# A two-block kernel with another order of its second block, a joint compression and longer value-product runs

## The chip, the cores and the metric

One core of a Trainium2 chip runs the whole program in one launch. The metric is the device time of one execution in microseconds (us). TensorE (PE) does matrix products and transposes, VectorE (DVE), ScalarE (ACT) and GpSimd (POOL) the elementwise work, and SyncE (SP) issues nearly all DMAs. PEld is the weight-load side of TensorE: a matmul's stationary operand is loaded there while an earlier matmul still runs.

## What is computed

The input is 512 tokens of 1024 features, in float32. Two transformer-like blocks follow one another. The reference, cut to what matters here:

```python
def reference(x, ...):
    x = first_block(x, ...)
    return second_block(x, ...)

# first_block
    xn = rms_norm(h, mix_norm[l])
    proj = jnp.einsum("bsd,dp->bsp", xn, w_in[l]) + b_in[l]
    q, k, v, cb, cc, cx, ga, gc = jnp.split(proj, splits, axis=-1)
    attn = sliding_window_attention(q, k, v, sinks[l])
    conv = cb * causal_depthwise_conv(cc * cx, conv_w[l])
    merged = (jax.nn.sigmoid(ga) * jnp.einsum("bsc,cd->bsd", attn, w_attn_branch[l])
              + jax.nn.sigmoid(gc) * jnp.einsum("bsc,cd->bsd", conv, w_conv_branch[l]))
    h = h + jnp.einsum("bsd,de->bse", merged, w_out[l])
    # then h = h + feed-forward part, with a depthwise convolution, and rms_norm

# second_block
    h = x @ w_in[l]                       # 33 projections of up to 128 columns
    o_nsa = nsa_mixer(...)                # 6 heads: compressed, selected and window branch
    o_sb = stick_breaking_mixer(...)      # 4 heads
    o_hg = hgrn2_mixer(...)               # 6 heads, a gated recurrence
    mixed = jnp.concatenate([o_nsa * silu(nsa_z), o_sb * silu(sb_z), o_hg * silu(hg_z)], axis=-1)
    x = layer_norm(ALPHA * x + mixed @ w_out[l], ln_g[l], ln_b[l])

# nsa_mixer
    def compress(src, w1, w2):            # src: keys or values, 31 blocks of 32 tokens
        blocks = src[:, blk_idx] + cmp_pos
        return gelu(blocks.reshape(..., 32 * dk) @ w1) @ w2
    kc, vc = compress(kc_src, w_ck1, w_ck2), compress(vc_src, w_cv1, w_cv2)
    # each branch: softmax(q k^T + bias) v, then
    return gb[..., 0:1] * o_c + gb[..., 1:2] * o_s + gb[..., 2:3] * o_w
```

## The kernel before, in words

**Tiling.** Features lie on the 128 partitions and the 512 tokens on the free axis. A dense projection (`dense`, L218) makes one 128x512 tile from 8 blocks of 128 input features. Float32 is split in a high and a low part, so that each block costs three matmuls of 512 columns: high weights times high and low input (`wh`), low weights times high input (`wl`); 24 matmuls for a projection. The weights of a projection come as one 512 KB DMA into `raw` (two buffers), ScalarE casts them to `wh` (L196), VectorE subtracts to get `wl` (through `tt`, L136). `Weights.take` has the load four projections ahead of use and the splitting two ahead.

**The stages**, in time from the start of the span: the first block's 34 input projections with its attention (12 to 165 us), branches and output (165 to 272), the feed-forward part (272 to 673), and the second block: 33 projections (673 to 1007), during which all of its three mixers run, then the transposes of the residual (to 1014) and the output products (1015 to 1060).

**Streams in the second block.** The mixers are Python generators that emit instructions and yield estimated costs. `drive` (L165) always advances the stream that stands lowest in cost divided by its rate: the projections (`in_proj2`, rate 1), `stream_a` (recurrences and stick-breaking heads one after another as in `SEQ`, slowed by `RATE_A`), `sparse` (compression, then the 24 units of the sparse attention, slowed by `RATE_B`) and `finishing` (the products with the gates). `ORDER` is the order of the 33 projections and `KORD` that of the last eight, the gates z. Each engine runs its instructions in the order so emitted, apart from places marked with a priority: weight splitting is lifted by 100 places, and `run` (L141) emits a list of matmuls as one block that waits for all of its inputs.

**Names.** Projections: `gf gq gi` of the recurrence (three pairs of heads), `nq` the sparse queries (three pairs), `kc vc` the keys and values to compress, `ks vs kw vw` those of the selected and window branches, `ng` their gates, `bq bk bv` the stick-breaking heads (two pairs). PSUM tiles: `pm` two banks for dense work, `pga` and `pgb` two each for scores and transposes, `poa` and `pob` one each for results. SBUF tiles are named by pools of 128x512 buffers: `nk`, `dk`, `hk`, `lv`, `np`, `gp`, `bi`, `r`.

**Matmul shapes.** Heads are 64 wide. Value products put the two heads of a pair in the two column halves of TensorE (`128*64` in the rows: 64 output partitions), all other products use its whole width (`128*128`).

**Compression before.** `compress` (L840) is called for keys and again for values: four loads of 256 KB bring the first weight `w1` into `nk` tiles, 8 additions on VectorE (L857) build the blocks, and 16 float32 matmuls with `w1` stationary and 62 columns moving (31 blocks of two groups) make the hidden layer, followed by a gelu on small tiles. `compressed` (L882) then applies `w2`, and for each of 4 query tiles makes scores of 6 heads with 31 keys, in float32, a softmax, and transposes. The results are `kcT` and `vcn`.

**One unit of the sparse attention before** is a pair of heads j, a query tile i and a branch br: `nsa_a` makes scores and softmax (L942, L948, L955), and while the next unit's scores are emitted `nsa_b` (L958) transposes the probabilities into `pgb` (L965), copies them to SBUF (L967, one on VectorE, one on ScalarE), and emits the value products into `pob` as one `run` (the compressed branch's two products go with br 0). The first block's attention (`softmax_a`, `softmax_b`, L457 and L493) works in the same way for units (j, ip), with one run of value products for each.

## Time and profile before

| | |
|---|---|
| time, median of 3 runs | 1068.86 us (1068.28 to 1069.32) |
| the profiled execution's own time | 1068.53 us |
| its span | 1066.8 us |
| granted TensorE clock, mean | 0.999 |
| TensorE busy | 1039.5 us, 97% |
| VectorE busy | 704.4 us, 66% |
| ScalarE busy | 488.8 us, 46% |
| GpSimd busy | 44.0 us, 4% |

1.7 us of the profiled time lie outside the span. Busy time is the union of an engine's records; a TensorE record's end is modelled and reaches past the start of the next one, so that "busy" tells that work is queued, not that the array runs at its peak. What a matmul costs in a row of others is read from the distance of starts. A wait of PEld can still be covered by a matmul that runs; idle time of PE cannot.

### The profile page before, as it was taken

What the parts mean: (1) busy time and instruction counts of PE and PEld (TensorE: products, weight loads), DVE (VectorE), ACT (ScalarE), POOL (GpSimd) and SP (SyncE); (2) the same over time, 40 slices, a digit from 0 to 9 for tenths busy, and PEclk for the clock granted to TensorE, in tenths of its full rate; (3) what the DMA queues carried; (4) which work ended last, traced back from release to release, by engine and by line L of the source; (5) the groups of instructions that cost most, each with busy time, mean ns of one, the idle gap of its engine ahead of it and who ended that gap; (6) DMA issues with size and microseconds to landing.
All of it is one profiled execution on the core that took longest, in us unless ns stands there. A gap on an engine that the chain in (4) does not pass through costs nothing.

```text
span 1066.8 us, 14636 instructions
## 1 busy us (share of the span) xinstructions
PE 1039.5 (97%) x5712; PEld 838.9 (79%) x5712; DVE 704.4 (66%) x1313; ACT 488.8 (46%) x855; POOL 44.0 (4%) x89
## 2 busy tenths in 40 slices
PE   8999999999999999999999999999999999989997
PEld 6788888888888888888877888767777777767886
DVE  6876643356448777777763233597967698887757
ACT  5754443322344444444442222433625676578740
POOL 0000000000220000000000111200000000011000
PEclk9999999999999999999999999999999999999999
DMA  6212232333432233223335333531321110101232
GB/s 218 79 60 80 79 94 85 99 99 109 142 120 85 98 99 99 98 99 99 99 94 193 97 106 90 184 101 41 99 75 47 59 41 22 41 21 37 82 120 79
DMA packets 32801, 97.84 MB, mean 92 GB/s; under 512 B 4878, under 2 KB 5390, under 8 KB 32732
## 3 DMA queue, kind: packets, MB, share of 16 engines
q1 hardware_dynamic: 32732, 96.91, 28.7%
q8 instruction: 45, 0.74, 0.3%
q14 instruction: 24, 0.20, 0.1%
HBM read 94.77 MB, written 5.27 MB: 94 GB/s over the span
## 4 chain that ended last, share of the span: by engine, by line
PE 75%; DVE 11%; ACT 7%; DMA 3%; issue 2%; SPq 1%; POOL 1%; DVEq 0%; POOLq 0%; ACTq 0%
PE pm L139 44%; PE pob L139 12%; PE poa L139 12%; PE pga L139 4%; PE pgb L139 3%; DVE wl L136 2%; DMA raw<-in_w_in 1%; ACT wh L196 1%; DVE lv L136 1%; DMA raw<-in_w_down 1%; DVE hk L136 1%; DVE dk L136 1%; DVE np L136 1%; DVE nk L942 1%; ACT nk L948 1%
## 5 line engine op out<-in xcount | busy, mean ns | idle before, releaser
L139 PE MATMUL pm<-x,wh 128*128 128x512 f32 (+1 forms) x1360 | 433.4, 395 | 2.1 <-DVE x L133 0.9
L139 PEld LDWEIGHTS pm<-x,wh 128*128 128x128 f32 (+1 forms) x1360 | 252.2, 187 | 58.5 <-issue 3.5
L196 ACT CAST wh<-raw 128x1024 fp32r<-128x1024 f32 (+1 forms) x153 | 156.7, 1025 | 275.8 <-issue 109.9
L139 PE MATMUL pm<-x,wl 128*128 128x512 f32 (+1 forms) x680 | 268.3, 395 | 0.0
L136 DVE TENSOR_TENSOR wl<-raw,wh 128x1024 fp32r<-128x1024 f32 (+1 forms) x153 | 181.9, 1189 | 89.5 <-ACT wh L196 87.7
L139 PEld LDWEIGHTS pm<-x,wl 128*128 128x128 f32 (+1 forms) x680 | 127.0, 187 | 26.8 <-issue 1.6
L139 PE MATMUL poa<-x,wh 128*128 128x512 f32 x208 | 65.0, 394 | 0.0
L139 PE MATMUL pob<-x,wh 128*128 128x512 f32 x208 | 64.1, 390 | 0.0
L139 PE MATMUL pm<-np,wh 128*128 128x512 f32 x176 | 54.1, 389 | 0.0
L136 DVE TENSOR_TENSOR dk<-pm,rs 128x512 f32<-128x512 f32 x43 | 29.5, 686 | 28.1 <-PE pm L139 28.0
L139 PEld LDWEIGHTS poa<-x,wh 128*128 128x128 f32 x208 | 39.0, 188 | 9.3 <-issue 1.0
L139 PEld LDWEIGHTS pob<-x,wh 128*128 128x128 f32 x208 | 39.0, 188 | 8.0
L136 DVE TENSOR_TENSOR nk<-pm,rs 128x512 f32<-128x512 f32 x34 | 23.4, 687 | 32.6 <-PE pm L139 32.4
L139 PE MATMUL poa<-x,wl 128*128 128x512 f32 x104 | 40.6, 390 | 0.1
L139 PE MATMUL pob<-x,wl 128*128 128x512 f32 x104 | 40.6, 390 | 0.0
L139 PEld LDWEIGHTS pm<-np,wh 128*128 128x128 f32 x176 | 33.0, 188 | 6.8
L139 PE MATMUL pm<-np,wl 128*128 128x512 f32 x88 | 34.2, 389 | 0.0
L948 ACT ACTIVATE nk<-nk,q 128x128 f32<-128x128 f32 (+3 forms) x48 | 26.5, 555 | 11.5 <-DVE q L946 11.2
L942 DVE CUSTOM_DVE_ANT_0 nk<-pgb,bi 128x128 f32<-128x128 f32 (+3 forms) x48 | 23.1, 484 | 7.9 <-PE pgb L139 7.2
L133 DVE SCALAR_TENSOR_TENSOR dk<-nk,smt,dk 128x511 f32<-128x511 f32 (+1 forms) x34 | 25.4, 748 | 1.4 <-ACT dk L435 0.8
L139 PE MATMUL pgb<-np,np 128*128 128x128 f32 (+3 forms) x96 | 25.9, 351 | 0.4 <-DVE nk L967 0.3
L133 DVE SCALAR_TENSOR_TENSOR nk<-nk,smt,nk 128x511 f32<-128x511 f32 (+2 forms) x33 | 24.7, 747 | 0.5
(498 smaller groups left out, 1664.7 us busy)
## 6 DMA issues: line engine op xcount, KB each, us to landing
raw<-in_w_in SPq DMA_DIRECT2D x65, 512.0 KB, 3.5
raw<-in_w_up SPq DMA_DIRECT2D x44, 512.0 KB, 3.5
raw<-in_w_down SPq DMA_DIRECT2D x16, 512.0 KB, 3.6
raw<-in_w_br SPq DMA_DIRECT2D x8, 512.0 KB, 3.4
raw<-in_w_out SPq DMA_DIRECT2D x8, 512.0 KB, 3.5
raw<-in_w_out SPq DMA_DIRECT2D x16, 256.0 KB, 2.7
raw<-in_w_down SPq DMA_DIRECT2D x8, 384.0 KB, 3.2
d<-d SPq DMA_DIRECT2D x6, 512.0 KB, 6.6
```

The costliest lines, as they stand in the source:

```text
L133: V.scalar_tensor_tensor(o, i0, s, i1, op0, op1)
L136: V.tensor_tensor(o, i0, i1, op)
L139: return TE.matmul(o, l, r, start=start, stop=stop)
L196: A.copy(wh[:, c], raw[:, c])
L942: V.tensor_tensor_reduce(pb[:, 0:Wd_], s[:, 0:Wd_], bias[h][:, T - Wd_:T], 1.0, -3e38, ALU.add, ALU.max, st[:, g:g + 1])
L948: A.activation(pbs[g][:, 0:Wd_], pbs[g][:, 0:Wd_], AF.Exp, bias=st[:, 2 + g:3 + g], accum_out=st[:, 4 + g:5 + g])
```

## The change

1. **Order.** `ORDER`, `KORD` and the driver are new. `in_step` takes the projections as a clock (5.2 units of cost are one projection), and each stream has a first and a last projection in `PLAN` between which its cost is spread evenly. The three pairs of the sparse attention (`sparse(j)`) are three streams now, and the finishing steps come as streams at the end.
2. **Compression.** `blocks` (in place of `compress`) brings the weights, now into `np` tiles, and builds the blocks; `compressed` does the hidden layer of keys and values together: the block columns are stationary (64 wide), `w1` moves with 128 columns, keys go to the lower and values to the upper column half, 32 matmuls in one `run`. The gelu is done once on 128x128, and a transpose brings the result back. The compressed keys are kept split as high and low part side by side (`kc2`, 62 wide), and the scores use the queries' high and low parts as fp32r, all six heads of a query tile in one PSUM bank, with one more addition on VectorE.
3. **Value products.** `nsa_c` emits those of both branches and the compressed one in one `run` for each (j, i): 12 runs for 24. `softmax_c` does the same for the two units of a pair in the first block: 4 runs for 8. The copies of the first block now go to `lv` tiles, and some gates and merged tiles lie in other pools for that.

The diff, cut to its core:

```diff
-RATE_A = [0.593, 0.587, 0.591, 0.741, 0.778]
-RATE_B = [0.318, 0.367, 0.286, 0.332, 0.497]
-ORDER = [('gf', 0), ('gq', 0), 'kc', ('gi', 0), 'ng', 'vc', ('nq', 0), ('gf', 1), ('gq', 1), ('nq', 2), 'kw', 'ks', 'vs', ('bq', 0), ('gi', 1), ('gf', 2), 'vw', ('bk', 0), ('nq', 1), ('bv', 0), ('gq', 2), ('gi', 2), ('bq', 1), ('bk', 1), ('bv', 1)]
-KORD = [6, 5, 7, 0, 3, 1, 4, 2]
+ORDER = [("gf", 0), ("gq", 0), ("gi", 0), "ng", "kc", "vc", ("nq", 0), ("nq", 1), ("nq", 2), "ks", "vs", "kw", "vw",
+         ("gf", 1), ("gq", 1), ("gi", 1), ("bq", 0), ("bk", 0), ("bv", 0), ("gf", 2), ("gq", 2), ("gi", 2),
+         ("bq", 1), ("bk", 1), ("bv", 1)]
+PLAN = {("g", 0): (3, 9), ("g", 1): (16, 20), ("b", 0): (19, 24), ("g", 2): (23, 28), ("b", 1): (27.5, 32.5),
+        "c": (6, 12.5), ("n", 0): (13, 19.5), ("n", 1): (19.5, 26), ("n", 2): (26, 32.5)}
+KORD = [3, 0, 1, 5, 6, 7, 4, 2]
...
+    def in_step(clock, *streams):
...
+            for s in sorted(live, key=lambda s: s[3] + (s[4] - s[3]) * s[1] / s[2]):
+                g, did, work, first, last = s
+                if running and now < first + (last - first) * did / work:
+                    break
...
+                now += c / 5.2
...
-    def softmax_b(j, ip, po, sbs, lo):
+    def softmax_b(j, ip, sbs, lo):
...
-            pT = wk()
+            pT = tl("lv")
...
+    def softmax_c(po, held):
+        todo = []
+        for i, sblk, hh, w, first, last in held[0][0] + held[1][0]:
+            r = 64 * hh
+            todo.append(later(po[r:r + 64, i * P:(i + 1) * P], vn[:, sblk * P + r:sblk * P + r + 64], w, first, last))
+        run(todo, held[0][1] + held[1][1])
+        yield 2.0
...
-    def compress(name, w1name, w2name):
-        w1 = [nk().rearrange("p (k h) -> p k h", k=4) for _ in range(4)]
+    def blocks(name, w1name, w2name):
+
+        w1 = [np_().rearrange("p (k h) -> p k h", k=4) for _ in range(4)]
...
-        for k in range(16):
-            mm(ps[:, 0:62], w1[k // 4][:, k % 4], blks[k // 8][:, 62 * (k % 8):62 * (k % 8) + 62], k == 0, k == 15)
...
+        wk1, wk2, bk, e0 = yield from blocks("kc", "w_ck1", "w_ck2")
+        wv1, wv2, bv, e1 = yield from blocks("vc", "w_cv1", "w_cv2")
+
+        ps = bank("gb")
+        todo = []
+        for k in range(16):
+            c = slice(62 * (k % 8), 62 * (k % 8) + 64)
+            for r, w1, blks in ((0, wk1, bk), (64, wv1, bv)):
+                todo.append(later(ps[r:r + 64, 0:P], blks[k // 8][:, c], w1[k // 4][:, k % 4], k == 0, k == 15))
+        run(todo, [e0, e1])
...
+        TE.transpose(ps[:, 0:P], y, ident)
+        A.copy(yT, ps[:, 0:P])
...
+        A.copy(kc2[:, :, 0:31], kv)
+        tt(kc2[:, :, 31:62], kv, kc2[:, :, 0:31].bitcast(F32), ALU.subtract)
...
-                    mm(ps[:, 32 * h:32 * h + 31], pr["nq", h][g][:, i * P:(i + 1) * P].bitcast(F32), kcT[:, g, 0:31])
-                tt(pv[:, 3 * g:3 * g + 3], ps[:, 0:96].rearrange("p (h n) -> p h n", n=32)[:, :, 0:31],
-                   biasc[i][:, 3 * g:3 * g + 3], ALU.add)
+                    n = 64 * (3 * g + h)
+                    mm(ps[:, n:n + 62], pr["nq", h][g][:, i * P:(i + 1) * P], kc2[:, g, 0:62])
+            sv = ps[:, 0:384].rearrange("p (h n) -> p h n", h=6)
+            tt(pv, sv[:, :, 0:31], biasc[i], ALU.add)
+            tt(pv, pv, sv[:, :, 31:62], ALU.add)
...
+    def nsa_c(j, i, po, held):
+
+        todo, ends = [], []
...
+        for br, (pts, e) in enumerate(held):
+            vn_ = pr[("vs", "vw")[br]]
+            ends += e
+            for b in range(i + 1):
+                for g in range(2):
+                    r = 64 * g
+                    todo.append(later(po[r:r + 64, i * P:(i + 1) * P], vn_[:, b * P + r:b * P + r + 64],
+                                      pts[g][:, b * P:(b + 1) * P], False, br == 1 and b == i))
         run(todo, ends)
-        yield 0.16 * (i + 1)
...
-    drive((in_proj2(), 1.0), (stream_a(), 1.0), (sparse(), 1.0), (finishing(KORD), 1.0))
+    plan = [((recurrence if kind == "g" else sticks)([c]), 12.6 if kind == "g" else 13.2, *PLAN[kind, c])
+            for kind, c in SEQ]
...
+    in_step(in_proj2(), *((chain(n), *plan[n][1:]) for n in range(len(SEQ))),
+            (compressed(), 6.8, *PLAN["c"]), *((sparse(j), 14.2, *PLAN["n", j]) for j in range(3)),
+            *((finishing(n), 1.0, len(ORDER) - 8.0, len(ORDER) + 0.0) for n in KORD))
```

What this does to the instructions is seen from how they stand on an engine. On TensorE, before, a unit of the sparse attention late in the second block: the transposes of the probabilities (`pgb<-cst,nk`), a few dense matmuls of a projection (`pm<-x`), scores of a later unit (`pgb<-np,np`), then the value products of branch 1 alone (`pob<-nk,np`, 64 wide). `nk_7469` and `nk_7476` are the copies of the two transposes.

```order
L965 MATMUL pgb_7464<-cst,nk_7154 128x128 x4
L139 MATMUL pm_8245<-x_4420,wh_8169 128x512
L965 MATMUL pgb_7471<-cst,nk_7159 128x128 x4
L139 MATMUL pm_8245<-x_4419,wl_8170 128x512
L139 MATMUL pm_8245<-x_4511,wh_8169 128x512
L139 MATMUL pm_8245<-x_4512,wh_8169 128x512
L139 MATMUL pgb_7766<-np_5941,np_5902 128x128
L139 MATMUL pgb_7766<-np_5943,np_5902 128x128
L139 MATMUL pm_8245<-x_4511,wl_8170 128x512
L139 MATMUL pob_6944<-nk_7469,np_6434 64x128
L139 MATMUL pob_6944<-nk_7476,np_6434 64x128
```

Six matmuls stand there between the second transpose and the products that need its copy; the products of branch 0 stood in a run of their own earlier.

On TensorE, after, a unit with two key blocks (query tile i = 1): the end of the last transposes, dense matmuls, then one run with the compressed products (`np,vcn`), those of branch 0 (`np_6002`) and of branch 1 (`np_6115`).

```order
L1020 MATMUL pgb_6332<-cst,nk_6241 128x128 x2
L141 MATMUL pm_6339<-x_4883,wl_6272 128x512
L141 MATMUL pm_6339<-x_4976,wh_6271 128x512
L141 MATMUL pm_6339<-x_4977,wh_6271 128x512
L141 MATMUL pob_6124<-np_5901,vcn_5082 64x128 x2
L141 MATMUL pob_6124<-nk_6284,np_6002 64x128
L141 MATMUL pob_6124<-nk_6289,np_6002 64x128
L141 MATMUL pob_6124<-nk_6284,np_6002 64x128
L141 MATMUL pob_6124<-nk_6289,np_6002 64x128
L141 MATMUL pob_6124<-nk_6330,np_6115 64x128
L141 MATMUL pob_6124<-nk_6335,np_6115 64x128
```

One run stands for two, and the copies of branch 0 (`nk_6284`, `nk_6289`), whose transposes stand some 25 rows higher, have another unit's scores and many dense matmuls behind them.

The other place is the compression, TensorE again. Before, keys: 16 float32 matmuls of 62 columns into one bank, in two halves with dense matmuls of the next projection (`pob<-x`) between, and the same again for values.

```order
L139 MATMUL pgb_5297<-nk_5287,nk_5151 128x62 x4
L139 MATMUL pgb_5297<-nk_5287,nk_5152 128x62 x4
L139 MATMUL pob_5341<-x_4697,wl_5258 128x512
L139 MATMUL pob_5341<-x_4790,wh_5257 128x512
L139 MATMUL pob_5341<-x_4791,wh_5257 128x512
```

After, keys (`np_5577` is their `w1`) and values (`np_5599`) alternate in the two halves of one run.

```order
L141 MATMUL pgb_5623<-np_5577,nk_5587 64x128
L141 MATMUL pgb_5623<-np_5599,nk_5611 64x128
L141 MATMUL pgb_5623<-np_5577,nk_5587 64x128
L141 MATMUL pgb_5623<-np_5599,nk_5611 64x128
L141 MATMUL pgb_5623<-np_5577,nk_5587 64x128
```

The run now stands as one piece of 32 matmuls, behind all 16 block additions. On SyncE's DMA queue, after, the loads of `w1` come ahead of the bias tiles (`bi`) and of the third projection's weights (`raw_5102`); before, the bias loads stood directly behind `raw_5100`, and `raw_5102` behind them.

```order
L220 DMA raw_5098<-in_w_in 128x1024
L884 DMA np_5577<-in_w_ck 128x512
L884 DMA np_5578<-in_w_ck 128x512
L220 DMA raw_5100<-in_w_in 128x1024
L884 DMA np_5579<-in_w_ck 128x512
L884 DMA np_5580<-in_w_ck 128x512
L884 DMA np_5599<-in_w_cv 128x512
L884 DMA np_5600<-in_w_cv 128x512
L861 DMA bi_5085<-d_4300 128x512
```

Six loads of 256 KB have moved ahead of `raw_5102`, and each `np` tile that they write must first be released by TensorE.

## Rows read from the trace of the kernel before

**Rows 1.** The page's engine summary: busy time, share of the span, instructions.
```profile
PE 1039.5 (97%) x5712; PEld 838.9 (79%) x5712; DVE 704.4 (66%) x1313; ACT 488.8 (46%) x855; POOL 44.0 (4%) x89
```
**Rows 2.** The view by stretches: busy time of engines, PEclk the granted clock.
```profile
core 0: us, PE busy (x) PEld busy (x) DVE busy (x) ACT busy (x) POOL busy (x), PEclk, DMA share, GB/s
673.00:690.00 17.00, 16.17 (x70) 12.73 (x69) 9.25 (x18) 9.23 (x14) 6.80 (x27) 1.00 0.64 213
690.00:1003.00 313.00, 300.85 (x2301) 232.09 (x2300) 255.13 (x626) 183.58 (x389) 12.10 (x34) 1.00 0.17 54
...
940.00:980.00 40.00, 35.12 (x234) 25.47 (x234) 30.85 (x81) 32.91 (x75) 7.04 (x16) 1.00 0.09 27
```
**Rows 3.** PEld's waits, 690 to 1003 us: total us, times, longest; 8 of 27 rows.
```profile
PEld pob L139 <- ACT nk L967: 7.4, 18, 1.2
PEld pgb L139 <- issue: 4.5, 20, 1.1
...
PEld pgb L965 <- DVE q L942: 2.8, 7, 0.5
PEld pm L139 <- issue: 2.7, 12, 0.3
PEld pgb L139 <- DVE nk L857: 2.5, 3, 1.4
...
PEld pgb L377 <- DVE dk L136: 1.9, 1, 1.9
...
PEld pgb L965 <- DVE nk L955: 1.6, 5, 0.5
...
PEld pgb L925 <- issue: 0.4, 1, 0.4
```
**Rows 4.** PE matmuls by shape, 670 to 1005: count, busy, mean ns, idle before.
```profile
L139 PE MATMUL pob<-nk,np 128*64 128x128 f32 x240 | 17.8, 278 | 0.1
...
L139 PE MATMUL pgb<-nk,nk 128*128 128x62 f32 x64 | 8.2, 278 | 2.1 <-DVE nk L857 1.3 <-issue 0.8
...
L139 PE MATMUL pgb<-kcT,np 128*128 128x31 f32 x48 | 6.2, 261 | 0.1
```
**Rows 5.** Timeline of PE, 694 to 703: start, duration; x16 is sixteen records.
```profile
695.33 2.00 PE L139 MATMUL pgb<-nk,nk 128*128 128x62 f32 x16 [0.95 <-DVE nk L857]
697.13 0.48 PE L139 MATMUL pob<-x,wl 128*128 128x512 f32 x1
...
697.91 0.39 PE L139 MATMUL pob<-x,wl 128*128 128x512 f32 x1
698.14 0.62 PE L139 MATMUL pob<-x,wh 128*128 128x512 f32 x2
```
**Rows 6.** Timeline, 929 to 935: copies of transposes and the run behind them.
```profile
931.46 0.68 DVE L967 COPY nk<-pgb 128x512 f32<-128x512 f32 x1
...
932.37 0.56 ACT L967 COPY nk<-pgb 128x512 f32<-128x512 f32 x1
...
932.98 0.85 PEld L139 LDWEIGHTS pob<-nk,np 128*64 128x64 f32 x16 [0.38 <-ACT nk L967]
932.99 1.09 PE L139 MATMUL pob<-nk,np 128*64 128x128 f32 x16
```
**Rows 7.** Timeline of PE, residual transposes: fp32r matmuls of 128 columns.
```profile
1010.82 0.61 PE L139 MATMUL pm<-trir,x 128*128 128x128 f32 x4
1011.26 0.61 PE L139 MATMUL pgb<-trir,x 128*128 128x128 f32 x4
```
**Rows 8.** The chain of waits at the second block's start: start, duration.
```profile
673.45 6.29 DMA raw<-in_w_in
...
680.91 1.23 DVE wl L136
```
**Rows 9.** Timeline of PE, 685 to 688: the first matmul of the third projection.
```profile
686.28 0.62 PE L139 MATMUL pm<-x,wh 128*128 128x512 f32 x2
```
**Rows 10.** PEld's waits, 36 to 130 us, the first block's attention.
```profile
PEld poa L139 <- ACT nk L503: 0.9, 2, 0.4
```

More of the change, by code (lines that the diff above doesn't have):

```diff
@@ L159, in need @@
             yield None
-    def paced(g, rate):
-        for c in g:
-            yield c if c is None else c / rate
+    def in_step(clock, *streams):
+        now = 0.0
+        live = [[g, 0.0, work, first, last] for g, work, first, last in streams]
+        running = True
+        while running or live:
+            moved = False
+            for s in sorted(live, key=lambda s: s[3] + (s[4] - s[3]) * s[1] / s[2]):
+                g, did, work, first, last = s
+                if running and now < first + (last - first) * did / work:
+                    break
+                try:
+                    c = next(g)
+                except StopIteration:
+                    live.remove(s)
+                    moved = True
+                    break
+                if c is None:
+                    if did == 0:
+                        s[3] = max(first, min(now, last - 1.0))
+                    continue
+                s[1] += c
+                moved = True
+                break
+            if moved:
+                continue
+            if not running:
+                raise RuntimeError("nothing can go on")
+            try:
+                c = next(clock)
+                while c is None:
+                    c = next(clock)
+                now += c / 5.2
+            except StopIteration:
+                running = False
     def drive(*tasks):
@@ L1001, in sparse @@
             prev = (un, new)
+        o = rt()
+        A.copy(o, po)
+        outs[j] = o
+        done.add(("nsa", j))
     ZP = [(0, 0), (1, 0), (2, 0), (1, 384)]
```

136 lines of the change are left out of this document (62 added, 74 removed).

## The prediction

> **What bounds the kernel now.** I read the engine summary first [rows 1]: TensorE is busy 1039.5 of 1066.8 us, VectorE 66%, the others less. So the time falls only by what leaves TensorE's stream, as work or as waiting. Then the view by stretches [rows 2], since the change touches mainly the second block: from 690 to 1003 us TensorE is busy 300.85 of 313 us at a granted clock of 1.00, so the clock gives nothing, and 12.15 us are idle by its own records. VectorE has 255 us of work there, ScalarE 184. Then the waits of the weight loads in the same stretch [rows 3]. Its rows that name another engine sum to 35.4 us (27 rows in all, the first, the last and six more shown) and those marked "issue" to 11.1 us. Both measures are bounds: a late weight load is partly covered by the matmul that still runs, and a matmul's modelled end hides part of an idle gap. So TensorE loses between 12 and 35 us to waits on other engines there; I use the middle, 24. The largest is the value product behind the copy of its transposed probabilities (7.4 us in 18 waits). The timeline shows why [rows 6]: the copies end at 932.14 and 932.93, the loads of the products had waited 0.38 us and start at 932.98.
>
> **The compression.** The 62-column float32 run starts at 695.33 and the next dense matmul at 697.13 [rows 5]: 1.80 us for 8 matmuls (16 records, since float32 makes two passes), 0.225 each. The group counts 64 records, so 32 matmuls [rows 4], 7.2 us. Afterwards 32 matmuls of 128 columns in two column halves. The form exists in the trace as the value product: 16 records take 1.09 us, one lasts 0.278 [rows 4, 6], so starts are (1.09 - 0.278) / 15 = 0.054 apart, 0.108 a matmul: 32 cost 3.5 us. The added transpose is one 128-column pass or two, 0.1 to 0.2. Together -3.6 us. The run now waits for all 16 block additions, but rows 3 already hold three waits for these (2.5 us); one wait of 2 to 4 us instead I count at nothing. What would cover it is the dense work of the projections that stands around it.
>
> **The compressed scores.** 48 records of 31 columns are 24 float32 matmuls [rows 4]. Their mean length is close to that of the 62-column form (261 against 278 ns), so I take the same 0.225, 5.4 us. Afterwards they are single-pass fp32r of 62 columns. The nearest row is the residual transposes, fp32r of 128 columns, four from 1010.82 to 1011.26, 0.11 each with a load for each [rows 7]: 24 cost 2.7 us, gain 2.7. If the pass followed its columns, half of that would do, gain 4.1. I take 2.7, since the load of 128 columns stays. The added VectorE addition (4 of them) is off TensorE's path.
>
> The Trainium skill ("TensorE: Matmul & The Clock Gate", Back-to-back issue gap) gives 81 ns for a load and a matmul of 128 columns in a sustained row; by that the gain would be 3.5 and the sum 0.8 us lower. Rows 7 show 110 ns for such pairs.
>
> **Entering and leaving 64-wide runs.** When a run of half-width matmuls ends, the next full-width load waits without any engine to blame: 20 "issue" waits of `pgb` cost 4.5 us, 0.22 each, 12 of `pm` 2.7 [rows 3]. On entering, I estimate that the last full-width matmul must end: it lasts 0.39 where the next one otherwise starts 0.23 later (697.91, 698.14) [rows 5], so 0.16. In the order of instructions the kernel has 37 such runs before and 22 after: 12 fewer from the joint products of the sparse attention, 4 fewer from those of the first block, one more from the compression. 15 fewer cost 15 x 0.22 = 3.3 if only leaving counts and 15 x 0.38 = 5.7 with both. I take 5.0.
>
> TensorE's work thus falls by 3.6 + 2.7 + 5.0 = 11.3 us, between 9.4 (small ends) and 13.4.
>
> **Waiting.** The new order puts more of TensorE's work between a producer and its consumer. I counted, in the order, the TensorE time that stands between the two, at the trace's durations. Transposes to value products (the copy takes 0.56 to 0.68 us [rows 6]): median 1.6 us before, 5.3 after, since the first branch's products wait for the second branch. Scores to transposes: 5.0 before, 8.9 after. Projection to its value transposes: 0.9 before, 3.4 or more after. The chain of the stick-breaking heads (scores, log, sums) gains least: its smallest cover goes from 4.9 to 6.0. So of the 35.4 us of rows 3's view, I let go: most of the 7.4 behind the copies (-6.4), half of the 4.4 that the transposes wait for softmax (L942, L955: -2.2), the value transposes' waits (1.9 and a smaller 1.0: -2.9), a third of some 9 in the stick-breaking heads (-3), and 2 of the rest: 16.5, or 47%. At the same share the middle reckoning of 24 gives -11.3 and the idle time of 12.15 gives -5.7. I take -11.5, between -5.7 and -16.5. After those, the waits that come last are those of the stick-breaking heads and of the recurrence, whose inner order is unchanged.
>
> In the first block one copy wait stands [rows 10], 0.9 us: -0.5.
>
> **DMA.** Six loads of 256 KB now stand ahead of the third projection's weights. At the 213 GB/s of that stretch [rows 2] these 1.5 MB take 7.4 us. Before, that load landed at 679.74 (673.45 + 6.29) and its split ended at 682.14 [rows 8], its first matmul starts at 686.28 [rows 9]: 4.1 us of slack. So the wait is at most 7.4 - 4.1 = 3.3 us if none of the six starts before the second block, and nothing if they run under the last of the feed-forward part, as the buffers come free there. I take +0.5, which leaves the cover in place.
>
> **Sum**, against the profiled execution's own 1068.53 us (0.3 below the median, which I neglect): 1068.5 - 11.3 - 11.5 - 0.5 + 0.5 = 1045.7. I say 1045.5. With the small ends, 1068.5 - 9.4 - 5.7 + 3.3 = 1056.7; with the large ones, 1068.5 - 13.4 - 16.5 - 0.9 = 1037.7.
>
> **Rivals.**
> *The waits stay (A).* VectorE and ScalarE run in order, and what TensorE no longer waits for in one place it waits for in the next, since the same elementwise work is to be done in less time. Then only the work goes: 1068.5 - 11.3 = 1057.2, between 1052 and 1063. For it: VectorE has 82% of the stretch by its records already (255 of 313), and in the 40 us from 940 TensorE was busy only 35.1 though no engine was full [rows 2]. Against it: the order spreads the elementwise work more evenly, so that in the last stretch before (bq, bk, bv 1 and the gates) less is crowded.
>
> The Trainium skill ("TensorEngine Tiling (Array Packing)", PSUM Bottleneck) says the same of column halves: the products get faster, the copies out of PSUM do not and may become the limit. Rows 3 agree in kind, 7.4 us behind such copies.
>
> *VectorE becomes the bound (B), slower than before.* With the stick-breaking and recurrent streams from the 14th projection on, VectorE's instructions of the four projections gq1 to bk0 sum, at the trace's durations, to 50.5 us and TensorE's to 39.5; from bq1 to bv1 to 44.4 and 37.6. Each next projection needs a `wl` of 1.23 us from VectorE [rows 8], lifted by 100 places only, so a late VectorE stops even the dense work. Price: in the 40 us from 940 TensorE was idle for 4.9 us [rows 2]; with the middle reckoning twice the idle time (24 for 12.15), it lost 9.8. If the last projections from gq1 on, 176 us of TensorE, all ran like that, they would lose 9.8 x 176 / 40 = 43 us; with 4 in the part before, 47 against 24 now, +23, and 1068.5 - 11.3 + 23 = 1080. It turns the change into a loss as soon as waits exceed 24 + 11.3 = 35 us. Against it: behind each crowded place comes one in which VectorE has less to do than TensorE, and from 690 to 1003 as a whole it has 58 us to spare [rows 2].
>
> *The change doesn't do what it says.* The merged runs and the joint compression stand in the order as written, so this can only hold for the covers, which is A.
>
> **Chances.** Forecast 1045.5 (1037.7 to 1052): 0.60. A (1052 to 1063): 0.27. B (above 1070.6): 0.07. Between A and B, within 0.2% (2.1 us, about what a measurement of this kernel can tell from no change): 0.05. Below 1037: 0.01. To leave out no more than 2 in 10 the range reaches to 1061: outside are B, the 0.05, about 0.03 of A and the end below, 0.16 in all. Faster 0.88, same 0.05, slower 0.07.
>
> **What would show it.** Work: a compression run of 32 matmuls in about 3.5 us, compressed scores in about 2.7, "issue" waits of the loads fewer by some 15. Waits: the row behind the copies nearly gone and the sum of named waits near 19 instead of 35; if it stays above 30, A holds. DMA: the third projection's first matmul directly behind the second. B would show as waits for `wl` or for stick-breaking tiles in the stretch from gq1 on, with VectorE above 90%. I am wrong if VectorE's order, not the distance on TensorE, sets when a copy is ready.

## The result, and the profile after

The changed kernel takes 1062.2 us (median of 4, 1061.65 to 1062.8) against 1069.07 us before (4 runs). The ratio is 0.993, 95% interval 0.9916 to 0.9944: faster by 0.7%. The prediction said 1045.5 us with a range up to 1061; the sign was right, the size a third of the forecast.

The engine summary of the changed kernel, to be read against [rows 1]:

```profile
PE 1028.5 (97%) x5689; PEld 835.7 (79%) x5689; DVE 704.3 (66%) x1307; ACT 485.6 (46%) x854; POOL 47.4 (4%) x93
```

TensorE's busy time fell by 11.0 us, the span by 7.0 (1066.8 to 1059.8). So about 4 us of what left TensorE's stream came back as idle time (27.3 to 31.3 us). Where, is read from the start of two stages. The rows are of PE's timeline: the first dense matmul of the second block and the first matmul of the residual transposes behind it, before and after.

```profile
673.40 0.62 PE L139 MATMUL pm<-x,wh 128*128 128x512 f32 x2
...
1007.29 0.56 PE L139 MATMUL pga<-trir,x 128*128 128x128 f32 x4
```

```profile
671.24 0.62 PE L141 MATMUL pm<-x,wh 128*128 128x512 f32 x2
...
1001.03 0.56 PE L141 MATMUL pga<-trir,x 128*128 128x128 f32 x4
```

The first block gave 2.2 us. The second block's projections and mixers took 333.9 us before and 329.8 after, only 4.1 less. The rest, 0.7 us, lies in the tail.

The view by stretches of the changed kernel, with the 313 us of [rows 2] first:

```profile
690.00:1003.00 313.00, 295.72 (x2308) 231.72 (x2305) 261.90 (x629) 186.57 (x398) 15.64 (x34) 0.99 0.17 53
712.00:732.00 20.00, 15.19 (x117) 11.63 (x116) 15.69 (x29) 3.71 (x8) 0.00 (x0) 0.91 0.15 51
728.00:730.00 2.00, 1.90 (x22) 1.90 (x24) 0.04 (x1) 0.00 (x0) 0.00 (x0) 0.64 0.00 0
730.00:732.00 2.00, 2.00 (x23) 2.00 (x20) 0.00 (x0) 0.00 (x0) 0.00 (x0) 0.51 0.00 0
```

TensorE is idle for 17.3 us of the same 313 where it was idle for 12.15, and one stretch of 20 us alone holds 4.8 of them, with the granted clock at 0.91. It holds the start of the joint compression, whose wait is 3.2 us, and one wait of 1.3 us in the first recurrence. PE's timeline of the compression (start, duration; in brackets the idle time before, and what ended it), and the VectorE row that it waits for:

```profile
724.49 0.40 PE L141 MATMUL pm<-x,wl 128*128 128x512 f32 x1
728.10 5.38 PE L141 MATMUL pgb<-np,nk 128*64 128x128 f32 x64 [3.21 <-DVE nk L899]
```

```profile
723.41 4.64 DVE L899 TENSOR_TENSOR nk<-nk,smt 64x248 f32<-64x248 f32 x8
```

The run waits for the last of 8 block additions in a row, 3.2 us, and then 32 matmuls take 5.38 us instead of the 3.5 forecast. The clock granted after the idle time is 0.64 and then 0.51 in the two stretches of 2 us, down to the level of 1.2 GHz; at a granted clock of 1.00 the same run later takes 3.71 us (`later_compression`, below).

The waits of the weight loads from 671.5 to 1000.5 us, to be read against [rows 3] (total us, times, longest):

```profile
PEld pm L141 <- issue: 4.9, 19, 0.6
PEld pga L141 <- ACT hk L1100: 4.1, 4, 1.4
PEld pob L141 <- ACT nk L1022: 3.9, 7, 1.6
PEld pga L141 <- DVE lv L138: 3.8, 8, 1.0
PEld pgb L141 <- DVE nk L899: 3.6, 1, 3.6
...
PEld poa L141 <- POOL hk L1069: 3.1, 2, 1.6
...
PEld pgb L1020 <- DVE nk L1010: 1.0, 3, 0.7
```

The waits behind the copies of the transposed probabilities went from 7.4 us in 18 to 3.9 in 7, as meant. The transposes' waits for the softmax fell too. But the stick-breaking heads (L1100 is the cast of their logs, L1069 their mask on GpSimd, `lv L138` the sum of their logs) wait longer than before, and the sum over all rows that name an engine (the named waits, from here on), in the whole second block, is 37.5 us in 61 waits where it was 40.0 in 91. The same sum over the waits of TensorE's own records rose, from 11.4 to 17.6. There are fewer waits and larger ones.

### The profile page after: what moved, and what is told of

Same layout as the page of the kernel before. It is cut to its first block, busy times and chain, and to the rows that moved or that the text cites. A ratio compares the mean times of both kernels' runs of the same rounds, so it can differ in the third digit from the quotient of the medians.

```text
span 1059.8 us, 14588 instructions
## 1 busy us (share of the span) xinstructions
PE 1028.5 (97%) x5689; PEld 835.7 (79%) x5689; DVE 704.3 (66%) x1307; ACT 485.6 (46%) x854; POOL 47.4 (4%) x93
## 4 chain that ended last, share of the span: by engine, by line
PE 73%; DVE 14%; ACT 6%; DMA 2%; issue 2%; POOL 1%; SPq 1%; POOLq 0%; DVEq 0%; ACTq 0%
PE pm L141 44%; PE poa L141 12%; PE pob L141 11%; PE pgb L141 3%; PE pga L141 2%; DVE wl L138 2%; DVE lv L138 2%; DVE dk L138 2%; DVE hk L138 1%; ACT wh L230 1%; DMA raw<-in_w_down 1%; DVE r L138 1%; DVE nk L1010 1%; DVE nk L899 1%; DVE nk L997 1%
## 5 line engine op out<-in xcount | busy, mean ns | idle before, releaser
L141 PE MATMUL pm<-x,wh 128*128 128x512 f32 x1360 | 435.2, 397 | 1.9 <-ACT x L287 1.0
L141 PEld LDWEIGHTS pm<-x,wh 128*128 128x128 f32 x1360 | 252.0, 189 | 56.2 <-issue 4.9
L230 ACT CAST wh<-raw 128x1024 fp32r<-128x1024 f32 (+2 forms) x153 | 156.5, 1024 | 256.7 <-issue 102.5
L141 PE MATMUL pm<-x,wl 128*128 128x512 f32 x680 | 268.3, 395 | 0.0
L138 DVE TENSOR_TENSOR wl<-raw,wh 128x1024 fp32r<-128x1024 f32 (+2 forms) x153 | 182.0, 1190 | 88.0 <-ACT wh L230 85.0
L141 PEld LDWEIGHTS pm<-x,wl 128*128 128x128 f32 x680 | 128.2, 188 | 27.5 <-issue 1.9
L141 PE MATMUL pob<-x,wh 128*128 128x512 f32 (+1 forms) x208 | 64.9, 392 | 0.0
L138 DVE TENSOR_TENSOR dk<-pm,rs 128x512 f32<-128x512 f32 x43 | 29.5, 685 | 25.9 <-PE pm L141 25.8
L138 DVE TENSOR_TENSOR nk<-pm,rs 128x512 f32<-128x512 f32 x35 | 24.0, 686 | 32.1 <-PE pm L141 31.9
L141 PEld LDWEIGHTS pob<-x,wh 128*128 128x128 f32 (+1 forms) x208 | 37.6, 181 | 9.6 <-issue 0.2
L141 PE MATMUL pob<-x,wl 128*128 128x512 f32 (+1 forms) x104 | 40.5, 389 | 0.0
L1003 ACT ACTIVATE nk<-nk,q 128x128 f32<-128x128 f32 (+3 forms) x48 | 26.5, 554 | 11.3 <-DVE q L1001 11.2
L135 DVE SCALAR_TENSOR_TENSOR nk<-dk,smt,nk 128x511 f32<-128x511 f32 (+2 forms) x33 | 24.7, 747 | 0.8 <-ACT nk L469 0.3
```

Source lines behind the costliest of these rows:

```text
L135: V.scalar_tensor_tensor(o, i0, s, i1, op0, op1)
L138: V.tensor_tensor(o, i0, i1, op)
L141: return TE.matmul(o, l, r, start=start, stop=stop)
L230: A.copy(wh[:, c], raw[:, c])
L1003: A.activation(pbs[g][:, 0:Wd_], pbs[g][:, 0:Wd_], AF.Exp, bias=st[:, 2 + g:3 + g], accum_out=st[:, 4 + g:5 + g])
```

## Experiments

Two theories stood at first. **O:** the new order itself adds waiting, because it puts the elementwise work of several streams side by side. **P:** the joint pieces add it, each at its place, since each waits for the last of several inputs. All times are medians; the runs come in four groups, in which the kernel before measured 1068.85 to 1070.31, so a difference of about 1 us between kernels of two groups can't be told. Every trace is one execution.

### The code and the order apart

`new_code_old_order` is the changed code under the tables and the driver of before:

```diff
-    in_step(in_proj2(), *((chain(n), *plan[n][1:]) for n in range(len(SEQ))),
+    drive((in_proj2(), 1.0), (stream_a(), 1.0), (stream_b(), 1.0), (ends(KORD), 1.0))
```

> The changed kernel's code (joint compression, joint value products in both blocks) with the order, the rates and the driver of the kernel before. Theory O (the new order itself adds waiting: it puts the elementwise work of several streams into the same stretches and VectorE, in order, falls behind): the work saved stays (first block 2.2 us, second block's matmuls about 7, mode changes about 4) and the waits stay as before, so 1068.9 - 13 = about 1056 us. Theory P (the joint pieces themselves add waiting, since each waits for the last of several inputs): the waits rise here too, 1060 to 1063.

Measured: 1085.07 us, ratio 1.0141 (1.0107 to 1.0175). Both theories missed. From 920 to 940 us, by the view by stretches and PE's waits there:

```profile
920.00:940.00 20.00, 13.24 (x211) 10.96 (x209) 12.24 (x41) 5.09 (x16) 0.00 (x0) 0.76 0.00 1
```

```profile
PE pgb L1022 <- DVE nk L1012: 3.2, 1, 3.2
PE pgb L1022 <- DVE q L999: 2.6, 2, 2.2
```

TensorE is idle a third of this stretch, no other engine is full and no weights come in: there is no dense work between the steps of the sparse attention, so that their latency stands open, and the clock falls to 0.76 besides. The old rates do not fit the new code, so this run can't tell O from P.

`old_code_new_order` goes the other way:

```diff
-                if br == 1:
-                    yield from nsa_c(j, i, po, held)
-                    held = []
+                yield from nsa_c(j, i, po, held, br)
+                held = []
```

with `compress` and the first block's value products as before.

> The old code of the compression and of the value products (one run for each branch and unit) in the new order with the new driver. Theory O: waits up by 6 us or more at unchanged work, 1073 to 1078 us. Theory P: the new order alone is no worse or better, 1064 to 1069.

Measured: 1065.14 us, ratio 0.9959 (0.9945 to 0.9973). Theory O falls: the order alone gains 4 us. PEld's named waits are 32.8 us in 65 against 40.0 in 91. But TensorE's idle time in the second block did not fall. The view by stretches, from the first dense matmul to the residual transposes: the kernel before, this one, and the changed kernel (length, PE busy):

```profile
673.40:1007.29 333.89, 320.92 (x2385) 248.05 (x2384) 267.53 (x649) 195.78 (x408) 18.90 (x61) 1.00 0.20 63
673.39:1004.55 331.16, 318.17 (x2385) 248.10 (x2384) 272.69 (x656) 195.93 (x414) 19.54 (x60) 1.00 0.21 65
671.24:1001.03 329.79, 311.14 (x2363) 243.48 (x2361) 270.31 (x647) 195.23 (x412) 21.98 (x64) 0.99 0.19 60
```

Idle are 13.0, 13.0 and 18.7 us. The 2.7 us that the order gains in this stretch are busy time; why the same matmuls are busy for less is open.

### The first block

`first_block_only` (second block in old code and old order, sparse attention as three generators):

> Only the first block's joint value products (4 runs for 8); second block in old code and old order. Both theories: the second block started 2.2 us earlier in the changed kernel's trace, so about 1066.7 us; if that was chance of the schedule, 1068.9.

Measured: 1070.15 us, ratio 1.0006 (0.999 to 1.0021). Its second block starts at 671.14 us, so the 2.2 us are there, but it then takes 337.5 us, 3.6 more than before. I had rewritten the sparse attention's stream there, and it no longer makes the next pair's scores ahead; so the run is confounded and was repeated on the kernel before itself:

```diff
+    def softmax_c(po, held):
...
-                yield from softmax_b(j, ip, po, *args)
+                held.append((yield from softmax_b(j, ip, *args)))
```

> The kernel before, its second block untouched, with only the first block's joint value products (and the buffers they need). In four traces the second block starts at 671.0 to 671.3 us with them and at 673.4 without, so 1066.7 us. If the second block gives the gain back (its schedule starts from another state of buffers), 1068 to 1069.

Measured: 1067.17 us, ratio 0.999 (0.9979 to 1.0001), some 1.7 us less. Its second block starts at 671.19. The first block's gain of about 2 us stands in every trace that has the edit; in time the interval still reaches no change.

### The compression's place

The order is built by a planner that puts an instruction where its own model of time has its inputs ready. In the order, emitting the run later did not move it (no run was made of that), so I bound it behind ScalarE's work for the projection nq 0:

```diff
+        yield from need(("nq", 0))
+        e2 = last_act().name
...
-        run(todo, [e0, e1])
+        run(todo, [e0, e1, e2])
```

> The changed kernel with the joint compression run standing about 35 instructions later, behind the evacuation of the projection nq 0. In the changed kernel TensorE stood idle for 3.2 us before this run and the run went at a granted clock of 0.5 to 0.6 for 4 us. Theory P (loss of the place): both go, about 5 us, 1057 us. Theory O (VectorE is late in the whole stretch): the wait appears again behind VectorE in the next place and only the slower clock's 1.9 us are won, about 1060.5.

Measured: 1057.06 us, ratio 0.9883 (0.9845 to 0.992). PE's timeline of this kernel:

```profile
731.43 3.71 PE L141 MATMUL pgb<-np,nk 128*64 128x128 f32 x64 [0.61 <-ACT np L419]
```

The run takes 3.71 us now and waits 0.61. Theory P holds for this place: of the 5 us, 2.6 lay in the wait itself and 1.7 in the clock behind it. Two edits on top of this kernel ask what the joint runs and the first recurrence beside the compression cost:

The first, `later_split_runs`, makes one run for each branch again:

```diff
-                if br == 1:
-                    yield from nsa_c(j, i, po, held)
+                yield from nsa_c(j, i, po, held, br)
```

> The kernel of later_compression with the sparse attention's value products again in one run for each branch (24 runs for 12). If joint runs pay by mode changes alone: 12 runs x 0.35 = 4 us more, 1061. If, as its trace suggests, the joint runs lose part of that again because each waits for the last copy of the second branch (two waits of 1.3 us in front of them), 1058 to 1059.

Measured: 1058.26 us, ratio 0.9891 (0.9874 to 0.9907). The second block of this kernel, then of `later_compression`:

```profile
670.93:996.85 325.92, 312.55 (x2362) 241.06 (x2361) 272.67 (x650) 196.48 (x413) 19.90 (x64) 1.00 0.20 62
670.99:996.28 325.29, 309.43 (x2362) 241.73 (x2361) 270.92 (x647) 195.40 (x412) 21.44 (x64) 1.00 0.19 61
```

Joining the runs saves 3.1 us of TensorE's busy time there (3.7 in the whole span) and adds 2.5 us of idle time (13.4 to 15.9): the second of the two expectations, and theory P again.

The second, `later_adds_on_gpsimd`:

```diff
-                    last = V.tensor_tensor(
+                    last = G.tensor_tensor(
```

> The kernel of later_compression with the 16 block additions of the compression on GpSimd instead of VectorE (9 us of VectorE work between the 4th and 7th projection moved to an engine that is idle there). Theory V: the waits of the first recurrence beside it (1.4 us at the 6th projection and smaller ones) go, 1055 us. Theory L: no change, 1057; if GpSimd is slow on these strided reads, the joint compression waits again and it is slower.

Measured: 1057.21 us, ratio 0.9879 (0.9865 to 0.9894). So the 12 joint runs of the sparse attention are worth about 1.2 us net, 0.1 for each run saved, hardly more than these runs can tell; and 9 us of VectorE's work (16 records) taken from beside the compression change nothing.

### Load, chain or cover

What sets the waits that are left? **V** and **A:** the queues of VectorE or ScalarE. **L:** the mixers' own chains of steps are longer than the TensorE work that stands between their ends. Three runs took load away, on top of `later_compression`:

`later_no_scale` leaves out:

```diff
-            V.tensor_scalar(pbs[g][:, 0:Wd_], pbs[g][:, 0:Wd_], st[:, 8 + g:9 + g], None, ALU.mult)
```

> The kernel of later_compression without the 48 multiplications by the softmax's scale on VectorE (the division by the sum and the gate are left out, so this part of the computation is missing): 17 us less VectorE work between the 13th projection and the end, TensorE's work as it was. Theory V (VectorE, in order, is late, and what waits for it is set by its queue, in the stick-breaking heads and the recurrence too): waits fall by 5 us or more there, 1050 us or less. Theory L (the heads' own chains of ScalarE, GpSimd and VectorE steps are longer than the cover, whatever stands in the queue): only the sparse attention's own waits fall, 1055 to 1056.

Measured: 1056.46 us, ratio 0.9873 (0.9858 to 0.9888).

`later_no_exp`:

```diff
-            A.activation(
-                pbs[g][:, 0:Wd_], pbs[g][:, 0:Wd_], AF.Exp, bias=st[:, 2 + g:3 + g], accum_out=st[:, 4 + g:5 + g]
-            )
+        V.memset(st[:, 4:6], 1.0)
...
-            V.tensor_scalar(pbs[g][:, 0:Wd_], pbs[g][:, 0:Wd_], st[:, 8 + g:9 + g], None, ALU.mult)
+            V.tensor_scalar(pbs[g][:, 0:Wd_], pbs[g][:, 0:Wd_], st[:, 8 + g:9 + g], -1.0, ALU.mult, ALU.max)
```

> The kernel of later_compression without the 48 exponentials of the sparse attention (this part of the computation is missing; the sums are set to one and the scaled values are cut at -1 so that all stays finite): some 35 us of ScalarE work gone from its queue between the 13th projection and the end, VectorE's and TensorE's work as before. Theory A (ScalarE, in order, is where the stick-breaking heads and the recurrence queue: in later_compression's trace a head's Abs, Exp and Ln stand between the exponentials of the sparse attention and the six of the recurrence's decay): waits of stick-breaking and recurrence fall by 4 us or more, 1051 us or less. Theory L (the chain itself is too long, with an empty queue too): only the sparse attention's own waits fall, 1054 to 1056.

Measured: 1058.71 us, ratio 0.9906 (0.9889 to 0.9922), not faster at all.

`later_copies_on_vector`:

```diff
-            ends.append((V.tensor_copy if g == 0 else A.copy)(pT[:, 0:Wd_], ps[:, 0:Wd_]))
+            ends.append(V.tensor_copy(pT[:, 0:Wd_], ps[:, 0:Wd_]))
```

> The kernel of later_compression with all 48 copies of transposed probabilities on VectorE instead of half of them on ScalarE: 10 us moved from ScalarE to VectorE. Theory A: fewer waits, 1055 to 1056. Theory L, or VectorE late after all: 1057 or slower, since two copies of a unit now run one after the other and the joint run waits for the second.

Measured: 1055.75 us, ratio 0.9876 (0.9861 to 0.9891).

Neither 17 us less on VectorE nor 35 us less on ScalarE (sums of records; the busy time fell by 14.7 and 24.8 us) gained more than these runs can tell: 0.6 us less and 1.7 more. The 1.3 us of the copies, 0.7 by the ratios, are at that limit too. PEld's named waits stay at 32.2 and 34.2 us without the scale and the exponentials, against 33.7. One caution: with less work the planner also puts TensorE's instructions earlier. The smallest TensorE time between scores and transposes in the order, 2.7 us in `later_compression`, is 0.5 in both. So these runs do not hold the cover fixed, and they show only that relief of a queue is not passed on to the time here.

`later_no_mask` shortens the chain, with GpSimd's selections left out:

```diff
-                            strict(e, ZP[jb][1])
...
-                            e = strict(zs[b], ZP[jb][1])
```

> The kernel of later_compression without the masks that GpSimd applies in the stick-breaking heads (32 selections of 0.3 to 0.6 us, twice in each chain; the causal mask on the diagonal blocks is missing): the chain from scores to value products is one engine shorter at two places. Theory L: the waits behind ScalarE's cast (2.5 us) and behind GpSimd (1.7 us) mostly go, 1053 to 1054 us. Theory A: the cast still queues on ScalarE, only GpSimd's 1.7 us go, 1055.5.

Measured: 1054.02 us, ratio 0.9859 (0.9844 to 0.9874), 3 us less. PE's waits of it hold neither the cast of the heads nor their masks:

```profile
PE pga L141 <- DVE lv L138: 2.2, 5, 1.1
PE pob L141 <- ACT nk L1024: 2.2, 2, 1.2
PE pga L141 <- DVE hk L1231: 1.5, 2, 1.3
PE pgb L141 <- POOL nk L328: 1.4, 1, 1.4
```

The next edit lengthens the smallest cover, the TensorE work between a block's scores and the sum that first needs it, and leaves the steps of the chain and the load as they are. A head makes scores in three blocks and then three sums; the first sum needed the block made last.

```diff
-                for b in range(3):
+                for b in (1, 2, 0):
                     zb = bank("ga")
...
-                for b in range(3):
+                for b in (2, 1, 0):
                     cb = bank("ga")
```

> The kernel of later_compression with the three blocks of scores of a stick-breaking head made in the order 1, 2, 0 and their sums in the order 2, 1, 0, so that the first sum no longer needs the scores made last. In the order, the smallest TensorE time between scores and sums goes from 6.0 to 9.8 us, the median from 9.9 to 13.1; work, load and chain are as before. If the smallest cover decides: the waits behind ScalarE's cast (2.5 us) and most of those behind the sums' subtraction go, 1054 to 1055 us. If the waits move on to the next consumer as they did when load was taken off: 1056.5 to 1057.

Measured: 1054.76 us, ratio 0.9861 (0.9847 to 0.9876). The wait behind the heads' cast, in PE's waits from 671 to 996 us, first `later_compression`, then this kernel:

```profile
PE pga L141 <- ACT hk L1102: 2.5, 3, 1.0
PE poa L141 <- POOL hk L1071: 1.7, 2, 1.1
PE pga L141 <- DVE hk L1237: 1.5, 2, 1.3
PE pga L141 <- DVE lv L138: 1.4, 4, 0.7
```

```profile
PE pgb L1022 <- DVE q L999: 2.1, 1, 2.1
PE pob L141 <- ACT nk L1024: 1.9, 3, 1.2
...
PE pga L141 <- DVE lv L138: 0.6, 3, 0.2
...
PE pga L141 <- ACT hk L1102: 0.4, 1, 0.4
```

2.5 us became 0.4, `lv` 1.4 became 0.6, and one new wait of 2.1 us appeared elsewhere, a transpose in front of its softmax. Net 2.3 us.

That the smallest cover decides does not follow: the edit raised the median too, from 9.9 to 13.1 us. I count the covers of the twelve blocks of `later_compression` from PE's records, idle time left out: 6.2 to 17.8 us. Its three waits behind the cast (1.02, 0.71 and 0.74 us) stand at covers of 13.4, 8.5 and 12.9; the two smallest, 6.2 and 7.3, have none. ScalarE's timeline of the largest of these waits has the copy of the block's scores, its next step (Abs) and the cast:

```profile
850.24 0.59 ACT L1094 COPY lv<-pga 128x512 f32<-128x512 f32 x1
...
856.41 0.63 ACT L1095 ACTIVATE dk<-lv 128x512 f32<-128x512 f32 x1
...
863.95 0.62 ACT L1102 CAST hk<-dk 128x512 fp32r<-128x512 f32 x1 [1.12 <-POOL dk L1071]
```

```profile
864.62 0.44 PE L141 MATMUL pga<-hk,trir 128*128 128x384 f32 x1 [1.02 <-ACT hk L1102]
```

From copy to cast 14.3 us pass. The block's own steps on ScalarE, VectorE and GpSimd take 5.8 of them by their rows; for 5.6 us the Abs alone stands behind other streams' work in ScalarE's order. In `later_no_exp`, with less work there, ScalarE stands idle for 2.8 us at this place and the Abs starts even later, since the cast of the block before, which needs GpSimd's mask, and five other instructions come first in its order:

```profile
850.25 0.57 ACT L1091 COPY lv<-pga 128x512 f32<-128x512 f32 x1
...
854.26 0.62 ACT L1099 CAST hk<-dk 128x512 fp32r<-128x512 f32 x1 [2.82 <-POOL dk L1068]
...
857.56 0.62 ACT L1092 ACTIVATE dk<-lv 128x512 f32<-128x512 f32 x1
```

So at this place the chain is long through its place in ScalarE's order: its own steps (L) don't account for it, and less work in the queue (A) did not shorten it. The other waits were not followed like this.

### Three more

`later_recurrence_earlier` puts the second recurrence's projections first:

```diff
+ORDER = [("gf", 0), ("gq", 0), ("gi", 0), "ng", "kc", "vc", ("nq", 0), ("nq", 1), ("nq", 2), ("gf", 1), ("gq", 1), ("gi", 1),
+         "ks", "vs", "kw", "vw", ("bq", 0), ("bk", 0), ("bv", 0), ("gf", 2), ("gq", 2), ("gi", 2),
...
+PLAN = {("g", 0): (3, 9), ("g", 1): (12, 17), ("b", 0): (19, 24.5), ("g", 2): (23.5, 28), ("b", 1): (27, 32.5),
+        "c": (6, 12.5), ("n", 0): (16, 21.5), ("n", 1): (21.5, 27), ("n", 2): (27, 32.5)}
```

> The kernel of later_compression with the second recurrence's three projections ahead of the keys and values of the sparse attention, that recurrence between the 12th and 17th projection and the stick-breaking heads spread over 5.5 projections instead of 5. Projections 8 to 15 take 7 to 8 us each in later_compression's trace and 16 to 24 take 9 to 18, so the mixers crowd the second half. Theory V: spreading them lowers the waits, 1053 to 1055. Theory L: no change, 1057.

Measured: 1057.36 us, ratio 0.9882 (0.9867 to 0.9897): nothing. Its trace holds one new wait, in the last head, at a cover of 3.2 us, with a lower granted clock in the 4 us from 970 (PE's timeline, the view by stretches):

```profile
970.22 0.49 PE L141 MATMUL pga<-hk,trir 128*128 128x512 f32 x1 [3.35 <-ACT hk L1102]
```

```profile
970.00:974.00 4.00, 3.38 (x29) 2.96 (x29) 3.75 (x7) 4.00 (x9) 0.12 (x1) 0.66 0.21 66
```

So what the more even spread is worth without this wait is not shown.

`later_joint_runs` binds the joint runs further back:

```diff
+                    yield 0.6
+                    held[1][1].append(last_act().name)
                     yield from nsa_c(j, i, po, held)
```

> The kernel of later_compression with each joint run of the sparse attention emitted 0.6 units of cost later and bound behind the ScalarE work emitted by then; the TensorE time between transposes and value products goes from 2.1 to 3.4 us at the tenth percentile, from 5.6 to 7.7 in the median. If the smallest cover decides: the waits of 1.3 us in front of two of the runs go, 1055 us. If binding it behind ScalarE adds waits of its own, 1057 or slower.

Measured: 1061.29 us, ratio 0.9924 (0.9909 to 0.9938): 4 us slower. PE's waits in front of the runs went from 2.7 us to 0.8, but the largest wait of its trace stands in a stick-breaking head:

```profile
861.80 0.45 PE L141 MATMUL pga<-hk,trir 128*128 128x384 f32 x1 [1.72 <-ACT hk L1104]
```

In its order the smallest cover of the sums is 4.5 us where it was 6.0. But this wait stands at a cover of 10.3 us, and waits do not explain the 4 us at all: TensorE's idle time falls from 28.2 to 27.1 us, while its busy time rises from 1026.8 to 1032.5, 2.9 us of it in the value products of the sparse attention (17.3 to 20.2). Why is open.

`later_bias_copies` concerns a queue that the prediction did not look at. In the chain of waits of the changed kernel the bias tiles land at 672.7, and GpSimd copies from them ahead of its last addition of the norm's squares:

```profile
668.49 4.19 DMA bi<-d
...
672.73 3.77 POOL np L878 x18
...
676.94 1.23 POOL nk L328
...
678.22 1.14 PE pgb L141 x2
```

```diff
-                G.tensor_copy(v[:, h, 0:n], bias[h][:, o:o + 16 * (n - 1) + 1:16])
+                c = G.tensor_copy(v[:, h, 0:n], bias[h][:, o:o + 16 * (n - 1) + 1:16])
+                tc.add_manual_dep(c.ins, z, mybir.DependencyInfo(
```

> The kernel of later_compression with the 24 bias copies on GpSimd made to wait until the compression's blocks are begun. In the changed kernel 18 of them (3.8 us from 672.7) stand in front of the last addition of the norm's squares, and TensorE then waits 1.4 us for it (0.8 before). If this queue is the cause: 0.6 to 1.4 us less, 1056 us. If the norm waits for something else: 1057.

Measured: 1056.82 us, ratio 0.988 (0.9864 to 0.9897). The norm's matmul no longer waits in its trace, but a gain of 0.2 us is less than these runs can tell, so the queue is shown and its price is not.

`later_three_edits` puts the three edits together:

> The kernel of later_compression with the reordered sums, the later bias copies and all copies of transposed probabilities on VectorE (1.3 us by itself). If the gains add up: 1057.1 - 2.5 - 1 - 1.3 = 1052 us. If each only moves waiting elsewhere: 1055 to 1056.

Measured: 1053.46 us, ratio 0.985 (0.9836 to 0.9865), with the edits shown above. It is faster than both kernels, by 1.5% than the one before. Of the 4.8 us expected for the three, 3.6 came; by what the three measured alone (2.3, 0.2 and 1.3 us), that is nearly all.

## Why the prediction was wrong, point by point

TensorE's records split the sum, as far as their modelled ends allow. The work was forecast to fall by 11.3 us; busy time fell by 11.0, and by 12.7 with the compression's place mended (1.7 of that came with the order alone, which was not forecast). The waits were forecast to fall by 11.5; idle time rose by 4.0, and by 0.9 with the place mended. So the work was about right and the waits were wrong.

**The compression.** Predicted 3.5 us for 32 matmuls; 3.71 in `later_compression`, so the shape was sized well. In the changed kernel it took 5.38 after a wait of 3.2. The prediction counted "one wait of 2 to 4 us instead" at nothing, against three old waits of 2.5 us. The wait had the size named, but its cover was not there, and the granted clock behind it had not been thought of. This step failed: together 5 us, 2.8 of it idle time in the second block (18.7 us, 15.9 without it).

**The scores.** Predicted 0.11 us each. PE's timeline of the changed kernel:

```profile
761.84 0.83 PE L141 MATMUL pgb<-kc,np 128*128 128x62 f32 x6
```

With one record's mean of 0.274 us, (0.83 - 0.274) / 5 = 0.111. Right. The Trainium skill's 81 ns a pair for 128 columns ("TensorE: Matmul & The Clock Gate", Back-to-back issue gap) does not hold for this form, even at 62 columns; the measurement decides.

**Changes of mode.** Predicted 0.33 us a run, 5 us for 15. Splitting the 12 joint runs again raised TensorE's busy time by 3.7 us, 0.31 a run, so the price was sized well as work. What was missing is its other side: a joint run waits for the last copy of both branches, and 2.6 us of idle time went with the split, so that 1.2 us was left of the gain. The sign named for it, some 15 "issue" waits of the loads fewer, did not show in the sum (50 with 11.9 us before, 47 with 13.4 after), because the new order alone raised them to 56; splitting the 12 runs raised them from 48 to 58.

**The waits.** Predicted -11.5 us; this is the term that failed. The order alone left TensorE's idle time in the second block at 13.0 us; the joint runs of the sparse attention added 2.5 and the compression's place 2.8. Three steps in it were wrong. First, the cover was judged by its median, and a longer cover was taken for a shorter wait. The waits behind copies and softmax did fall, but TensorE then waited elsewhere: in the heads 3 us less was predicted, while their rows went up. Second, a cover was not set against the time that its chain takes. The chain of a head's block took 14.3 us where its own steps take 5.8, through its place in ScalarE's order; the prediction had named VectorE's order as its sign of being wrong, and here it is ScalarE's. Third, the share by which the loads' waits fell was carried over to TensorE's own loss. In `old_code_new_order` the loads' named waits fell by 7.2 us and the idle time by nothing: the two measures do not move together. The 35.4 us themselves came from a view cut at 27 of its 40 rows; all of them give 38.8, and 35.7 in the same stretch of the changed kernel, above the 30 that was named as the sign of A.

**First block and DMA.** Predicted about 2 us there with its share of the modes and the copy wait, and 0.5 lost to the loads. The first block gave 2.2 in the changed kernel's trace; the third projection's first matmul stands directly behind the second's (684.66 after 684.44), so the loads cost nothing. The bias tiles that now come behind those loads do delay the norm, through GpSimd's queue, by half a microsecond: PE's timeline has the norm's matmul, before and after, with 0.83 and 1.37 us of idle time ahead of it.

```profile
679.83 0.70 PE L139 MATMUL pgb<-dk,ones 128*128 128x512 f32 x1 [0.83 <-POOL dk L294]
```

```profile
678.22 1.12 PE L141 MATMUL pgb<-nk,ones 128*128 128x512 f32 x2 [1.37 <-POOL nk L328]
```

**The rivals.** A came closest: the work goes, the waits stay, 1057.2 us. The 5 us more are the compression's place, which A did not contain, and with that place mended the kernel measures 1057.06. That is partly luck: the work then falls by 1.4 us more than A had it, and the idle time rises by 0.9. B did not come. In four stretches of 20 us (from 692, 792, 812 and 892) VectorE is busy for over 97%, and TensorE is idle for only 0.7, 0.1, 1.4 and 1.5 us there; 17 us less of VectorE's work gained nothing that can be told. The Trainium skill's rule on PSUM ("TensorEngine Tiling (Array Packing)", PSUM Bottleneck), that tiling speeds up TensorE but not the copies out of PSUM, which may become the limit, agreed in kind with the waits behind copies. But all copies on one engine, 1055.75 us, cost no time, so how much the engines can copy is not what binds here.

What stays open: how much of the remaining waits is due to the engines' order. It is seen at one place, and the planner's earlier placing is seen in the order (2.7 to 0.5 us), but no run held the order fixed with less load, or changed ScalarE's order alone.

## What to carry to other kernels

Where one engine runs nearly all the time and waits in many small places, set for each producer and consumer pair the work that stands between them against the time that the chain really takes in the trace, with what stands in front of its steps on each engine; neither the median nor the smallest cover told where the waits would be. Ask of a joint step which single input comes last. Check the order for the planner's own idea of readiness: a dependency on a later instruction moved the run and gained 5 us. A cheap reordering inside one chain (the sums of a head) was worth 2.3 us, where a plan for all streams gave 4.

## What the hardware showed that was not expected

In a second block that otherwise keeps TensorE at a granted clock of 1.00, a wait of 3.2 us (with one of 1.3 us some 4 us before it) put the following 4 us at 0.64 and 0.51 and cost 1.7 us more on a run of 3.7: half of the wait again. In `later_recurrence_earlier` the 4 us from 970, where a wait of 3.35 us ends, were at 0.66, and in `new_code_old_order` a stretch of 20 us with waits of 2 to 3 us was at 0.76. Waits of 1.0 to 1.2 us in `later_compression` left the clock at 1.00 in the stretches looked at.
